# Attention values with a head's values stationary and normalised, turned probabilities moving

## The chip, the core and the metric

The kernel runs on one core of one Trainium2 chip. The time is device time in microseconds of one execution, and the figure of a kernel is the median of its runs. The engines are named as the profile names them: PE (matmuls; PEld is its weight load), DVE (vector), ACT (activation), POOL, and SP, which issues most transfers. A matmul holds one operand in the array (stationary) and streams the other through it (moving); its output goes to PSUM, which has eight banks of 128 partitions x 512 fp32 columns. DVE and ACT read PSUM and SBUF; POOL works in SBUF alone.

## The reference

Two layers of an encoder block on one sequence of 512 tokens of width 1024. Each layer is a half-weighted SwiGLU, a mixing part, a second half-weighted SwiGLU and a final norm. The mixing part projects the normed input once and splits the columns: one group is latent attention with 8 heads (queries and keys of 96, values of 64 per head, mask by chunks of 64 tokens), the other a gated causal convolution of 31 taps over 512 channels with a layer norm. Both are joined and projected back. What the change touches is this:

```
for i in range(s // Q_BLOCK):                       # Q_BLOCK = 128
    q0 = i * Q_BLOCK
    k_end = q0 + Q_BLOCK
    scores = einsum('bhqd,bhkd->bhqk', q[:, :, q0:k_end], k[:, :, :k_end]) * scale
    scores = where(k_chunk[None, :] <= q_chunk[:, None], scores, -1e30)
    probs = softmax(scores, axis=-1)
    outs.append(einsum('bhqk,bhkd->bqhd', probs, v[:, :, :k_end]))
x = x + concatenate([attn, conv], axis=-1) @ w_out
```

## The kernel before

The residual x lies in SBUF with features on partitions: eight tiles of 128 features x 512 tokens. The large products split each fp32 operand into a rounded high part and a low rest, and take three matmuls (`mm3`, L139 to L142) in place of one; `split` (L144) makes the two parts, the high one on ACT (L146), the low one on DVE (L147).

In `mix_body` the attention is cut into stages per head, and `ORDER = "t0s1p3v4o5"` gives each stage its lag in heads: at each step of the loop at L686 head h is turned (t), head h-1 scored (s), head h-3 has its probabilities turned (p), head h-4 its values taken (v), and head h-5 its output turned (o).

- `turn` (L604): queries and keys of a head, tokens on partitions, are transposed on PE to features on partitions, and copied out of PSUM by ACT (L609) and DVE (L614).
- `scores` (L617): for each of the four blocks of 128 queries one fp32 matmul against the 128, 256, 384 or 512 keys up to the block's end (L630), a small matmul that adds the mask (L631), the negated row maximum on DVE (L632), and the exponential on ACT (L636), which also adds up each row's sum. The probabilities are not divided by that sum here. They lie with queries on partitions, 1280 elements wide for a head over the four blocks.
- `turn_p` (L641): ten transposes on PE (L651) put keys on partitions; the results are copied to SBUF (L654), by DVE twice and by ACT once.
- `values` (L657): for each query block the turned probabilities are the stationary side (128 keys x 128 queries) and a head's 64 value columns move (L664): ten products per head, into a bank that two heads share by columns. Queries are on partitions, so the row sums are factors per partition: after the second head of a pair DVE takes reciprocals (L669) and multiplies the bank by them (L671) on the way to SBUF.
- `turn_out` (L675): four transposes on PE (L682) put the pair's 128 features on partitions, and `split` makes the operands of the output projection.

The convolution runs beside the attention, channels on partitions, in four tiles of 128 channels. For tiles of kind "D" DVE does all 30 shifted taps (L703) into a PSUM accumulator, which ACT copies out at the end (L713); for tiles of kind "A" ACT multiplies (L707) and POOL adds (L711). POOL then sums the four tiles (L725 to L727) for the layer norm's mean, PE spreads that sum (L729), and the first groups of the output projection follow (`early_groups`).

The order of the instructions on each engine is set when the program is built: a scheduler with its own estimate of durations deals the recorded instructions out to the engines, which then run them strictly in that order, each waiting on semaphores for its operands. So the convolution's taps stand between the attention's instructions where the scheduler has put them.

Of the kernel before, what the change touches and what calls it, by code (L numbers as in the profile page):

```python
# [7 lines left out]
FP = mybir.dt.float32  # L8
# [4 lines left out]
ALU = mybir.AluOpType  # L13
AX = mybir.AxisListType

P = 128
D = 1024
S = 512
L = 2
KD = D // P  # L20
NT = S // P
# [4 lines left out]
DV = 64  # L26
# [23 lines left out]
WOG = 3  # L50
WOP = 4
EVP = "DAD"
ORDER = "t0s1p3v4o5"

VECS = [("g1", 8), ("gm", 8), ("g2", 8), ("gp", 8), ("gql", 3), ("gkl", 2),
        ("cw", 4 * CK), ("cb", 4), ("lg", 4), ("lb", 4), ("gq", 1), ("gk", 1)]
# [11 lines left out]
def encoder_kernel(ctx: ExitStack, tc: tile.TileContext, xT, consts, vecs, rgain, wgu1, wd1,  # L68
# [8 lines left out]
    small = ctx.enter_context(tc.tile_pool(name="small", bufs=2))  # L77
# [3 lines left out]
    def nm(s):  # L81
        uid[0] += 1
        return f"{s}{uid[0]}"

    def slot(dt=FP, w=S):
        return ring.tile([P, w], dt, tag="r", name=nm("r"))

    def tmp(w=S, dt=FP):
        return tmps.tile([P, w], dt, tag="t", name=nm("t"))

    def bank():
        return psum.tile([P, S], FP, tag="ps", name=nm("ps"))
# [4 lines left out]
    V, A, G, T = nc.vector, nc.scalar, nc.gpsimd, nc.tensor  # L97
# [9 lines left out]
    ident = cst[:, CID:CID + P]  # L107
# [36 lines left out]
    def split(src, w=S):  # L144
        hi, lo = slot(FR, w), slot(FR, w)
        A.copy(hi, src)  # L146
        V.tensor_tensor(lo, src, hi.bitcast(FP), ALU.subtract)  # L147
        return hi, lo
# [40 lines left out]
    def spread(r):  # L189

        dg = tmp()
        V.tensor_tensor(dg.rearrange("p (t j) -> p t j", t=NT),
                        ident[:, None, :].to_broadcast([P, NT, P]),
                        r[:, :, None].to_broadcast([P, NT, P]), ALU.mult)
        ps = bank()
        T.matmul(ps, ones, dg, start=True, stop=True)
        return ps
# [214 lines left out]
    def mix(l, gx, norm, done):  # L412
        with tc.tile_pool(name="k", bufs=4) as kpool:
            mix_body(kpool, l, gx, norm, done)

    def mix_body(kpool, l, gx, norm, done):
# [25 lines left out]
        cqT, ckT, pq, scqs, vs = [], [], [], [], []  # L442
# [155 lines left out]
        at = []  # L598
# [3 lines left out]
        heads = [{} for _ in range(H)]  # L602
# [14 lines left out]
        def scores(h):  # L617
            qT, kT = heads[h]["qk"]
            b01, b2, b3 = bank(), bank(), bank()
            if h % 2 == 0:  # L620
                heads[h]["sums"] = small.tile([P, NT, 2], FP, tag="sums", name=nm("sums"), bufs=3)
            sums = heads[h - h % 2]["sums"]
            mx = small.tile([P, NT], FP, tag="mx", name=nm("mx"), bufs=3)
            pi = []
            ps = [slot() for _ in range(3)]
            ps = [ps[0][:, 0:128], ps[0][:, 128:384], ps[1][:, 0:384], ps[2]]
            for i in range(NT):
                n = (i + 1) * P
                o = (b01[:, 0:128], b01[:, 128:384], b2[:, 0:384], b3)[i]
                T.matmul(o, qT[0:DQ, i * P:(i + 1) * P], kT[0:DQ, 0:n], start=True, stop=False)  # L630
                heads[h]["s"] = T.matmul(o[:, n - 64:n], mrow, mneg, start=False, stop=True).ins  # L631
                V.tensor_reduce(mx[:, i:i + 1], o, axis=AX.X, op=ALU.max, negate=True)  # L632
                p = ps[i]
                if QFOLD:
                    V.tensor_tensor(mx[:, i:i + 1], mx[:, i:i + 1], scqs[i][:, h:h + 1], ALU.mult)
                A.activation(p, o, AF.Exp, bias=mx[:, i:i + 1], scale=scqs[i][:, h:h + 1] if QFOLD else 1.0,  # L636
                             accum_out=sums[:, i, h % 2:h % 2 + 1])
                pi.append(p)
            heads[h]["p"] = pi

        def turn_p(h):  # L641
# [15 lines left out]
        def values(h):  # L657

            if h % 2 == 0:
                heads[h]["po"] = bank()  # L660
            po = heads[h - h % 2]["po"].rearrange("p (t h d) -> p t h d", t=NT, h=2)
            for t in range(NT):
                for j in range(t + 1):
                    T.matmul(po[:, t, h % 2], heads[h]["pt"][j][:, (t - j) * P:(t - j + 1) * P],  # L664
                             vs[j][:, h * DV:(h + 1) * DV], start=j == 0, stop=j == t)
            if h % 2 == 0:
                return
            rs = small.tile([P, NT, 2], FP, tag="rs", name=nm("rs"))
            V.reciprocal(rs, heads[h - 1]["sums"])  # L669
            o = tmp()  # L670
            V.tensor_tensor(o.rearrange("p (t h d) -> p t h d", t=NT, h=2), po,  # L671
                            rs[:, :, :, None].to_broadcast([P, NT, 2, DV]), ALU.mult)
            heads[h]["o"] = o

        def turn_out(h):  # L675

            if h % 2 == 0:
                return
            o = heads[h]["o"]
            ps = bank()  # L680
            for t in range(NT):
                T.transpose(ps[:, t * P:(t + 1) * P], o[:, t * P:(t + 1) * P], ident)  # L682
            at.append(split(ps))

        STAGES = [({"t": turn, "s": scores, "p": turn_p, "v": values, "o": turn_out}[c], int(d)) for c, d in zip(ORDER[::2], ORDER[1::2])]
        for step in range(H + 6):  # L686
            for stage, lag in STAGES:
                if 0 <= step - lag < H:
# [6 lines left out]
        for c in range(4):  # L695
# [4 lines left out]
            for k in range(CK - 2, -1, -1):  # L700
                s = CK - 1 - k
# [41 lines left out]
        for c in range(4):  # L743
            z = tmp()
            V.tensor_tensor(z, ys[c], pr, ALU.mult)
            s = tmp()
# [53 lines left out]
    for l in range(L):  # L800
# [46 lines left out]
        else:  # L847
# [3 lines left out]
            ps = spread(st3.token(D))  # L851
            for m in range(KD):
                o = slot()
# [83 lines left out]
```

## Time and profile before

| | |
|---|---|
| median of 3 runs | 1857.76 us (1856.42 to 1858.85) |
| span of the profiled execution, first to last instruction | 1857.6 us |
| PE busy | 1816.5 us (98%) |
| DVE busy | 1353.9 us (73%) |
| ACT busy | 935.7 us (50%) |
| POOL busy | 341.5 us (18%) |
| mean granted TensorE clock | 0.991 of full |

The span is the profiled execution's own time from its first to its last instruction; the runs are timed apart from it. A share of busy time is a mean over stages that have different limits: the two attention stages, one a layer, are about 60 us each, and the rest of the span is mostly the feed-forward products. A duration in a row is the instruction's own, and instructions of one engine overlap at their ends; how long one holds its engine is the time from its start to the next one's. In a chain of what ended last, the second column is that share already.

### The profile page before, as it was taken

What the parts mean: (1) busy time and instruction counts of PE and PEld (TensorE: products, weight loads), DVE (VectorE), ACT (ScalarE), POOL (GpSimd) and SP (SyncE); (2) the same over time, 40 slices, a digit from 0 to 9 for tenths busy, and PEclk for the clock granted to TensorE, in tenths of its full rate; (3) what the DMA queues carried; (4) which work ended last, traced back from release to release, by engine and by line L of the source; (5) the groups of instructions that cost most, each with busy time, mean ns of one, the idle gap of its engine ahead of it and who ended that gap; (6) DMA issues with size and microseconds to landing.
All of it is one profiled execution on the core that took longest, in us unless ns stands there. A gap on an engine that the chain in (4) does not pass through costs nothing.

```text
span 1857.6 us, 27862 instructions
## 1 busy us (share of the span) xinstructions
PE 1816.5 (98%) x11240; PEld 1623.6 (87%) x11240; DVE 1353.9 (73%) x1761; ACT 935.7 (50%) x1467; POOL 341.5 (18%) x242
## 2 busy tenths in 40 slices
PE   7999999999899999999999999999999999999997
PEld 6898989888688898989888999898978788989895
DVE  5985858678855985858679767675989569767674
ACT  4453535457944453535634535354679435535351
POOL 3000000238924000000310000002589310000002
PEclk9999999999999999999999999999999999999998
DMA  6142422424213142423512414123250322424221
GB/s 217 41 142 69 135 68 91 122 74 125 46 58 110 39 140 77 128 77 94 165 54 63 150 55 148 57 87 114 78 148 1 108 80 63 142 63 143 63 86 63
DMA packets 55569, 175.72 MB, mean 95 GB/s; under 512 B 6160, under 2 KB 6544, under 8 KB 55440
## 3 DMA queue, kind: packets, MB, share of 16 engines
q1 hardware_dynamic: 53856, 169.37, 29.3%
q0 software_dynamic: 1152, 4.19, 1.3%
q8 instruction: 88, 1.44, 0.3%
q10 hardware_dynamic: 432, 0.38, 0.1%
q14 instruction: 41, 0.34, 0.1%
HBM read 171.82 MB, written 2.10 MB: 94 GB/s over the span
## 4 chain that ended last, share of the span: by engine, by line
PE 82%; DVE 7%; POOL 4%; ACT 4%; issue 3%; DMA 0%; POOLq 0%; ACTq 0%; DVEq 0%
PE ps L140 26%; PE ps L142 26%; PE ps L141 25%; PE ps L664 2%; PE ps L630 1%; ACT pr L707 1%; POOL y L711 1%; DVE wl L135 1%; POOL acc L173 1%; DVE r L283 1%; PE ps L651 1%; DVE cv L703 1%; DVE t L288 1%; POOL sck L158 1%; ACT wh L129 1%
## 5 line engine op out<-in xcount | busy, mean ns | idle before, releaser
L141 PE MATMUL ps<-r,wh 128*128 128x256 f32 (+1 forms) x3280 | 1060.7, 325 | 2.3 <-DVE r L153 2.2
L140 PE MATMUL ps<-r,wh 128*128 128x256 f32 (+1 forms) x3280 | 1053.7, 328 | 8.9 <-ACT wh L129 7.9
L142 PE MATMUL ps<-r,wl 128*128 128x256 f32 (+1 forms) x3280 | 1052.7, 325 | 3.9 <-DVE wl L135 1.9
L140 PEld LDWEIGHTS ps<-r,wh 128*128 128x128 f32 x3280 | 621.4, 191 | 64.8 <-ACT wh L129 8.7
L141 PEld LDWEIGHTS ps<-r,wh 128*128 128x128 f32 x3280 | 625.8, 191 | 55.1 <-DVE r L153 3.2
L142 PEld LDWEIGHTS ps<-r,wl 128*128 128x128 f32 x3280 | 622.2, 191 | 56.8 <-DVE wl L135 4.4
L223 ACT CAST wh<-fr 128x1024 fp32r<-128x1024 f32 x216 | 226.9, 1051 | 318.1 <-PE ps L141 233.0
L129 ACT CAST wh<-raw 128x768 fp32r<-128x768 f32 (+4 forms) x214 | 187.7, 883 | 337.5 <-PE ps L141 170.0
L173 POOL TENSOR_TENSOR acc<-acc,t 128x512 f32<-128x512 f32 x52 | 89.4, 1725 | 1308.5 <-ACT t L172 1307.4
L225 DVE TENSOR_TENSOR wl<-fr,wh 128x1024 fp32r<-128x1024 f32 x216 | 263.8, 1222 | 79.6 <-ACT wh L223 76.6
L135 DVE TENSOR_TENSOR wl<-raw,wh 128x768 fp32r<-128x768 f32 (+4 forms) x198 | 209.5, 1063 | 125.9 <-ACT wh L129 124.5
L399 DVE SCALAR_TENSOR_TENSOR x<-ps,x 128x512 f32<-128x512 f32 x128 | 87.6, 687 | 119.1 <-PE ps L142 119.1
L711 POOL TENSOR_TENSOR y<-y,pr 128x509 f32<-128x509 f32 (+15 forms) x120 | 157.5, 1313 | 51.9 <-ACT pr L707 44.6
L703 DVE SCALAR_TENSOR_TENSOR cv<-r,vec,cv 128x511 f32<-128x511 f32 (+14 forms) x120 | 87.7, 731 | 3.1 <-ACT cv L699 1.7
L707 ACT ACTIVATE pr<-r,vec 128x511 f32<-128x511 f32 (+14 forms) x120 | 83.5, 722 | 8.2 <-POOL y L711 8.0
L223 ACT CAST wh<-raw 128x1024 fp32r<-128x1024 f32 x36 | 37.7, 1047 | 70.3 <-PE ps L141 70.3
L146 ACT CAST r<-t 128x512 fp32r<-128x512 f32 x96 | 55.7, 620 | 33.5 <-DVE t L260 20.6
L147 DVE TENSOR_TENSOR r<-t,r 128x512 fp32r<-128x512 f32 x96 | 64.7, 686 | 10.2 <-ACT r L146 10.2
L225 DVE TENSOR_TENSOR wl<-raw,wh 128x1024 fp32r<-128x1024 f32 x36 | 44.1, 1225 | 30.9 <-ACT wh L223 30.9
L630 PE MATMUL ps<-r,r 96*128 96x384 f32 (+3 forms) x128 | 47.8, 492 | 8.6 <-ACT r L609 4.4
L336 DVE TENSOR_TENSOR raw<-fr,fr 128x1024 f32<-128x1024 f32 x36 | 44.0, 1223 | 12.9 <-DMA fr<-in_wgu 12.9
L153 DVE SCALAR_TENSOR_TENSOR r<-x,vec,r 128x512 fp32r<-128x512 f32 x40 | 45.9, 1148 | 10.2 <-ACT r L152 10.2
(165 smaller groups left out, 1596.4 us busy)
## 6 DMA issues: line engine op xcount, KB each, us to landing
fr<-in_wgu SPq DMA_DIRECT2D x144, 512.0 KB, 3.6
raw<-in_wd SPq DMA_DIRECT2D x96, 384.0 KB, 3.1
raw<-in_wgu SPq DMA_DIRECT2D x32, 512.0 KB, 3.5
raw<-in_wd SPq DMA_DIRECT2D x32, 256.0 KB, 2.6
raw<-in_wcv SPq DMA_DIRECT2D x16, 512.0 KB, 3.6
raw<-in_wout SPq DMA_DIRECT2D x16, 512.0 KB, 4.5
wl<-in_wout POOLq DMA_DIRECT2D x8, 512.0 KB, 6.7
raw<-in_wql SPq DMA_DIRECT2D x6, 512.0 KB, 3.5
```

Source lines behind the costliest of these rows:

```text
L129: A.copy(hi[:, :w], raw[:, :w])
L135: (G if kind in POOLW.split() else V).tensor_tensor(lo[:, :w], raw[:, :w], hi[:, :w].bitcast(FP), ALU.subtract)
L140: T.matmul(o, lh, rh, start=first, stop=False, skip_group_check=free)
L141: T.matmul(o, lh, rl, start=False, stop=False, skip_group_check=free)
L142: T.matmul(o, ll, rh, start=False, stop=last, skip_group_check=free)
L173: (eng or (V if last else G)).tensor_tensor(self.acc, self.acc, sq, ALU.add)
L223: A.copy(hi[:, :w], src[:, :w])
L225: V.tensor_tensor(lo[:, :w], src[:, :w], hi[:, :w].bitcast(FP), ALU.subtract)
L399: V.scalar_tensor_tensor(x[:, m, :], pd, 0.5, x[:, m, :], ALU.mult, ALU.add)
L703: V.scalar_tensor_tensor(acc[:, s:], u[c][:, :S - s], tap(k), acc[:, s:], ALU.mult, ALU.add)
L707: A.activation(pr[:, s:], u[c][:, :S - s], AF.Copy, scale=tap(k))
L711: order["conv"] = G.tensor_tensor(acc[:, s:], acc[:, s:], pr[:, s:], ALU.add).ins
```

## The change

The division by the row sum moves to the front: right after a head's exponentials DVE takes the reciprocals of its four columns of sums (now one tile a head, no longer one a pair) and multiplies each of the four blocks of probabilities in place, in SBUF. Then the probabilities are turned as before. In `values` the roles are swapped: a head's 64 value columns of a key block are the stationary side, and the turned, normalised probabilities of that key block move, all query columns from the block's own to the last. The output has features on partitions: the first head of a pair writes partitions 0 to 63 of a bank, the second 64 to 127, in turns over the four key blocks. This is the layout that the output projection wants, so the multiplication on the way out, the stage `turn_out` and its four transposes per pair go, and `split` reads the bank at once. Nothing is done for the first head of a pair when its turn comes; both heads' products are issued at the second's.

```diff
-ORDER = "t0s1p3v4o5"
+ORDER = "t0s1p3v4"
...
-            if h % 2 == 0:
-                heads[h]["sums"] = small.tile([P, NT, 2], FP, tag="sums", name=nm("sums"), bufs=3)
-            sums = heads[h - h % 2]["sums"]
+            sums = small.tile([P, NT], FP, tag="sums", name=nm("sums"), bufs=3)
+            rs = small.tile([P, NT], FP, tag="rs", name=nm("rs"), bufs=3)
...
-                             accum_out=sums[:, i, h % 2:h % 2 + 1])
+                             accum_out=sums[:, i:i + 1])
                 pi.append(p)
+            V.reciprocal(rs, sums)
+            for i in range(NT):
+                V.tensor_scalar(pi[i], pi[i], rs[:, i:i + 1], None, ALU.mult)
             heads[h]["p"] = pi
...
             if h % 2 == 0:
-                heads[h]["po"] = bank()
-            po = heads[h - h % 2]["po"].rearrange("p (t h d) -> p t h d", t=NT, h=2)
-            for t in range(NT):
-                for j in range(t + 1):
-                    T.matmul(po[:, t, h % 2], heads[h]["pt"][j][:, (t - j) * P:(t - j + 1) * P],
-                             vs[j][:, h * DV:(h + 1) * DV], start=j == 0, stop=j == t)
-            if h % 2 == 0:
                 return
-            rs = small.tile([P, NT, 2], FP, tag="rs", name=nm("rs"))
-            V.reciprocal(rs, heads[h - 1]["sums"])
-            o = tmp()
-            V.tensor_tensor(o.rearrange("p (t h d) -> p t h d", t=NT, h=2), po,
-                            rs[:, :, :, None].to_broadcast([P, NT, 2, DV]), ALU.mult)
-            heads[h]["o"] = o
-
-        def turn_out(h):
-
-            if h % 2 == 0:
-                return
-            o = heads[h]["o"]
-            ps = bank()
-            for t in range(NT):
-                T.transpose(ps[:, t * P:(t + 1) * P], o[:, t * P:(t + 1) * P], ident)
-            at.append(split(ps))
+            po = bank()
+            for j in range(NT):
+                for e in (0, 1):
+                    T.matmul(po[e * DV:(e + 1) * DV, j * P:S], vs[j][:, (h - 1 + e) * DV:(h + e) * DV],
+                             heads[h - 1 + e]["pt"][j], start=j == 0, stop=j == NT - 1)
+            at.append(split(po))
```

Where the instructions stand is shown at three places of the first layer. Names are tiles: `mx` row maxima, `rs` reciprocals, `cv` the convolution accumulator in PSUM, `ps` a PSUM bank, `r` a tile of the ring in SBUF (probabilities, turned probabilities and values all lie there); the text ends with the output's partitions x elements.

DVE, around the turned copies of the second head, before:

```order
L654 COPY r_4616<-ps_4615 128x512
L654 COPY r_4630<-ps_4629 128x256
L703 SCALAR_TENSOR_TENSOR cv_5263<-r_4428,vec,cv_5263 128x497
L632 TENSOR_REDUCE mx_4595<-ps_4592 128x1
L703 SCALAR_TENSOR_TENSOR cv_5263<-r_4428,vec,cv_5263 128x496
L614 TENSOR_SCALAR r_4657<-ps_4652,vec 96x512
```

and now, where the scalings of the third head stand ahead of the same copies:

```order
L638 RECIPROCAL rs_4552<-sums_4551 128x4
L631 TENSOR_REDUCE mx_4616<-ps_4613 128x1
L688 SCALAR_TENSOR_TENSOR cv_5231<-r_4428,vec,cv_5231 128x499
L640 TENSOR_SCALAR r_4554<-r_4554,rs_4552 128x128
L640 TENSOR_SCALAR r_4554<-r_4554,rs_4552 128x256
L640 TENSOR_SCALAR r_4555<-r_4555,rs_4552 128x384
L640 TENSOR_SCALAR r_4556<-r_4556,rs_4552 128x512
L656 COPY r_4642<-ps_4641 128x512
L656 COPY r_4656<-ps_4655 128x256
L631 TENSOR_REDUCE mx_4616<-ps_4611 128x1
```

Each head has such a block of four scalings in a row, 32 a layer, among the convolution's taps, and the taps move later: the last one stood ahead of the copies of the sixth head, and stands behind those of the eighth now.

PE, the values of a pair. Before, a head's ten products, among them:

```order
L664 MATMUL ps_4634<-r_4200,r_4560 128x64 x2
L664 MATMUL ps_4634<-r_4227,r_4567 128x64
L664 MATMUL ps_4634<-r_4200,r_4560 128x64
L664 MATMUL ps_4634<-r_4227,r_4567 128x64
L664 MATMUL ps_4634<-r_4254,r_4574 128x64
```

and now both heads' products in one run:

```order
L666 MATMUL ps_4723<-r_4579,r_4200 64x512
L666 MATMUL ps_4723<-r_4642,r_4200 64x512
L666 MATMUL ps_4723<-r_4586,r_4227 64x384
L666 MATMUL ps_4723<-r_4649,r_4227 64x384
L666 MATMUL ps_4723<-r_4593,r_4254 64x256
L666 MATMUL ps_4723<-r_4656,r_4254 64x256
L666 MATMUL ps_4723<-r_4586,r_4281 64x128
L666 MATMUL ps_4723<-r_4649,r_4281 64x128
```

Twenty products with 64 moving columns have become eight with 128 to 512, in turns for the two heads.

DVE at the end of the attention, before:

```order
L671 TENSOR_TENSOR t_4956<-ps_4905,rs_4954 128x512
L654 COPY r_4959<-ps_4958 128x512
L654 COPY r_4973<-ps_4972 128x256
L147 TENSOR_TENSOR r_4994<-ps_4988,r_4993 128x512
L671 TENSOR_TENSOR t_5009<-ps_4977,rs_5007 128x512
L147 TENSOR_TENSOR r_5017<-ps_5011,r_5016 128x512
```

and now:

```order
L656 COPY r_4957<-ps_4956 128x512
L656 COPY r_4971<-ps_4970 128x256
L688 SCALAR_TENSOR_TENSOR cv_5231<-r_4428,vec,cv_5231 128x483
L688 SCALAR_TENSOR_TENSOR cv_5231<-r_4428,vec,cv_5231 128x482
L147 TENSOR_TENSOR r_4985<-ps_4975,r_4984 128x512
```

The last two taps have moved behind the last copies; on ACT the copy of their accumulator (L713 before, L698 now) stands behind the cast of the last pair's split.

More of the change, by code (lines that the diff above doesn't have):

```diff
@@ L659, in values @@
             if h % 2 == 0:
-                heads[h]["po"] = bank()
-            po = heads[h - h % 2]["po"].rearrange("p (t h d) -> p t h d", t=NT, h=2)
-            for t in range(NT):
-                for j in range(t + 1):
-                    T.matmul(po[:, t, h % 2], heads[h]["pt"][j][:, (t - j) * P:(t - j + 1) * P],
-                             vs[j][:, h * DV:(h + 1) * DV], start=j == 0, stop=j == t)
-            if h % 2 == 0:
-                return
-            rs = small.tile([P, NT, 2], FP, tag="rs", name=nm("rs"))
-            V.reciprocal(rs, heads[h - 1]["sums"])
-            o = tmp()
-            V.tensor_tensor(o.rearrange("p (t h d) -> p t h d", t=NT, h=2), po,
-                            rs[:, :, :, None].to_broadcast([P, NT, 2, DV]), ALU.mult)
-            heads[h]["o"] = o
-        def turn_out(h):
-            if h % 2 == 0:
-                return
-            o = heads[h]["o"]
-            ps = bank()
-            for t in range(NT):
-                T.transpose(ps[:, t * P:(t + 1) * P], o[:, t * P:(t + 1) * P], ident)
-            at.append(split(ps))
-        STAGES = [({"t": turn, "s": scores, "p": turn_p, "v": values, "o": turn_out}[c], int(d)) for c, d in zip(ORDER[::2], ORDER[1::2])]
+                return
+            po = bank()
[4 more added lines that the diff above has]
+            at.append(split(po))
+        STAGES = [({"t": turn, "s": scores, "p": turn_p, "v": values}[c], int(d)) for c, d in zip(ORDER[::2], ORDER[1::2])]
         for step in range(H + 6):
```

## The prediction

> **What bounds the kernel now.** I read the page first, then the two attention stages (about 470 to 531 us in the first layer, 1385 to 1445 us in the second): busy times by stretch, the chain that ended last inside them, and the order of time on DVE and POOL. From the page (busy us, share, instructions):
>
> ```profile
> span 1857.6 us, 27862 instructions
> PE 1816.5 (98%) x11240; PEld 1623.6 (87%) x11240; DVE 1353.9 (73%) x1761; ACT 935.7 (50%) x1467; POOL 341.5 (18%) x242
> ```
>
> PE bounds the whole, but the change lives in the attention stages, and there the shares are others. Stretches of them (start:end, length, busy us and instructions of each engine, then the granted clock):
>
> ```profile
> core 0: us, PE busy (x) PEld busy (x) DVE busy (x) ACT busy (x) POOL busy (x), PEclk, DMA share, GB/s
> 487.00:500.00 13.00, 12.75 (x95) 10.71 (x96) 12.34 (x25) 13.00 (x35) 12.22 (x10) 1.00 0.01 2
> 500.00:513.00 13.00, 13.00 (x99) 10.86 (x98) 12.55 (x26) 12.26 (x30) 12.28 (x10) 1.00 0.00 1
> 513.00:518.00 5.00, 5.00 (x37) 3.86 (x35) 5.00 (x11) 4.83 (x13) 4.70 (x4) 1.00 0.00 0
> 518.00:531.20 13.20, 12.41 (x111) 12.13 (x111) 5.49 (x11) 3.49 (x9) 3.93 (x4) 1.00 0.01 1
> ...
> 1413.00:1426.00 13.00, 13.00 (x99) 10.83 (x97) 12.88 (x26) 12.59 (x31) 12.27 (x10) 1.00 0.00 1
> ```
>
> Until 518 us PE, DVE, ACT and POOL are all within a few per cent of full: DVE is idle 0.66 + 0.45 + 0 us in 31. Only after 518 us has DVE room, 7.7 us. The second layer's row reads the same. The chain (start, us, engine and line) shows which of the full engines ends last:
>
> ```profile
> 499.88 0.49 PE ps L630 x2
> 501.29 0.22 PE ps L630 x2
> 501.54 0.73 PE ps L630 x2
> 502.30 0.94 PE ps L630 x2
> 504.40 2.18 PE ps L664 x20
> 507.10 0.47 PE ps L682 x4
> 529.87 0.70 DVE t L671
> 530.61 0.65 PE ps L682 x4
> ```
>
> It is PE row after row, with one step of DVE at the very end. So time taken from PE is worth something here only as long as DVE, nearly as full, does not grow.
>
> **The change on PE.** Removed per layer: eight times L664 at 2.18 us (an fp32 product is two instructions in the trace, so a head's ten products are x20), 17.4 us, and four times L682 at 0.47, 1.9 us: 19.3 together. Added for each head: four products with 512, 384, 256 and 128 moving columns. The fp32 scores L630 move just these widths: 0.94 + 0.73 + 0.49 + 0.22 = 2.38 us a head, 19.0 us a layer, if the array's two halves are used one after the other. No row shows products in different halves side by side; at best they cost half, 9.5 us, and PE sheds 9.8 us a layer. I take 19.0, by the nearest rows, and count PE's change (-0.3 us) as nothing. The Trainium skill, "TensorEngine Tiling (Array Packing)", Theoretical Speedup, puts a stationary side of at most 64 at up to 2x, which no run here shows; by that PE sheds the 9.8 us, and whether it shows in the time hangs on DVE.
>
> **The change on DVE, its own work.** Each head gets a reciprocal and four in-place scalings of 128, 256, 384 and 512 elements; each pair loses one L671 and its reciprocal. The prices: two copies of 512 and 256 elements up to the next start; L671 up to the next start; the smallest in-place scaling by a per-partition factor (L544, 8 elements) up to the next start; the reciprocals, with their mean in ns:
>
> ```profile
> 513.48 1.01 DVE L654 COPY r<-ps 128x512 f32<-128x512 f32 x2
> 514.41 0.72 DVE L703 SCALAR_TENSOR_TENSOR cv<-r,vec,cv 128x482 f32<-128x482 f32 x1
> 523.96 0.69 DVE L671 TENSOR_TENSOR t<-ps,rs 128x512 f32<-128x512 f32 x1 [0.74 <-PE ps L664]
> 524.57 1.01 DVE L654 COPY r<-ps 128x512 f32<-128x512 f32 x2
> ...
> 433.30 0.22 DVE L544 TENSOR_SCALAR ssh<-ssh,cq 128x8 f32<-128x8 f32 x1
> 433.43 0.54 DVE L542 TENSOR_REDUCE ssh<-t 128x4 f32<-128x384 f32 x1
> ...
> L669 DVE RECIPROCAL rs<-sums 128x8 f32<-128x8 f32 x4 | 0.8, 192 | 0.6 <-ACT r L636 0.6
> ```
>
> The copies hold DVE 0.93 us for 768 elements, so 1280 elements cost 1.55 us a head, 12.4 us a layer. The lower end is L544's 0.13 us for each of 32, 4.2 us. I take 12.4: the copies have the size, L544 hardly any data. Removed: 4 x 0.61 = 2.4. Four more reciprocals: at most 4 x 0.19 = 0.8. Own work: +10.8 us a layer (lower end +2.6). The Trainium skill, "VectorE: DVE Perf Modes", The perf-mode tier table, lets a scaling from SBUF to SBUF run fp32 at twice the rate that a PSUM operand allows; no row here shows one of size. By it the scalings would be 6.2 us, and the forecast near 1885 instead of 1898 us.
>
> **The change on DVE, its waits.** L544 is the same kind of instruction as the new scalings: in place in SBUF, with a factor per partition. Alone it took 0.22 us. Beside POOL's L711, and so its kin L578 and the two-input L581 (0.42 us alone), it did not:
>
> ```profile
> 427.16 2.60 POOL L711 TENSOR_TENSOR y<-y,pr 128x498 f32<-128x498 f32 x2
> 428.72 1.07 DVE L544 TENSOR_SCALAR ssh<-ssh,cq 128x8 f32<-128x8 f32 x1
> ...
> 449.75 0.42 DVE L581 TENSOR_TENSOR kn<-ck,scp 128x256 f32<-128x256 f32 x1
> ...
> 454.98 2.30 DVE L578 TENSOR_SCALAR scp<-sck,ratio 128x8 f32<-128x8 f32 x1 [1.53 <-POOL sck L158]
> 455.68 1.57 POOL L711 TENSOR_TENSOR y<-y,pr 128x496 f32<-128x496 f32 x1
> 457.20 0.68 DVE L579 TENSOR_TENSOR kn<-kn,sck 128x512 f32<-128x512 f32 x1
> 457.33 1.67 POOL L711 TENSOR_TENSOR y<-y,pr 128x495 f32<-128x495 f32 x1
> 457.80 1.48 DVE L581 TENSOR_TENSOR kn<-ck,scp 128x256 f32<-128x256 f32 x1
> ```
>
> L544 ended at 429.79, when POOL's pair did (429.76); L578 at 457.28, as POOL's 457.25. L579 slipped in before POOL's next, which then took 1.67 us, and L581 waited 1.06 us for that one. So they take turns. In the attention stage POOL runs one L711 after another, while L632, L654, L671 and L703 with a PSUM operand keep their lengths; before the change nothing of this kind stands there on DVE.
>
> ```profile
> 477.62 40.54 POOL L711 TENSOR_TENSOR y<-y,pr 128x511 f32<-128x511 f32 x31 [0.29 <-ACT pr L707]
> ...
> 1404.95 30.09 POOL L711 TENSOR_TENSOR y<-y,pr 128x504 f32<-128x504 f32 x23 [0.37 <-ACT pr L707]
> ```
>
> A turn of POOL is 40.54 / 31 = 1.31 us. Bounds of the waits: none, or 32 x 1.31 = 41.9 us a layer. My value: of a head's four scalings one slips in behind another, as L579 did, so three meet POOL. POOL has 12.22 + 12.28 + 4.70 + 3.93 = 33.1 us of work after 487 us; in a stage grown from 44 to some 64 us that is a share of 0.52. Who meets a turn midway waits half of it, who finds one queued all of it: about 1.0 us. 24 x 0.52 x 1.0 = 12.5 us. What stands behind the waiting scalings on DVE are the next head's maxima, which ACT's exponentials wait for, and copies of turned probabilities, which PE's values wait for; so the wait reaches both. POOL in turn is held by at most 12.4 us of scalings; the longer stage leaves it idle time for that, else its last sum moves by as much.
>
> **The room, and the sum.** DVE's idle time after 487 us is 8.8 us (above). But the new end needs part of it. Its steps: the last pair's values (2 x 2.38 = 4.8 us); then ACT's L146; behind it in ACT's order the copy of the last convolution accumulator, whose DVE taps now stand after the last turned copies; POOL's last sum; and only then PE's L729, which starts the next part:
>
> ```profile
> 515.36 0.58 ACT L713 COPY r<-cv 128x512 f32<-128x512 f32 x1
> 520.81 1.27 POOL L727 TENSOR_TENSOR t<-t,r 128x512 f32<-128x512 f32 x1
> 527.68 0.58 ACT L146 CAST r<-ps 128x512 fp32r<-128x512 f32 x1 [2.26 <-PE ps L682]
> 531.11 1.02 PE L729 MATMUL ps<-t,onesm 128*128 128x512 f32 x2
> ```
>
> That is 4.8 + 0.58 + 0.58 + 1.27 = 7.2 us, in which DVE works about 1.9 us (two taps, one split) and idles 5.3. Room: 8.8 - 5.3 = 3.5 us. The sum a layer: 10.8 + 12.5 - 3.5 = +19.8 us, with DVE in PE's place as the bound. Behind the stage PE is dense, so both layers' delays reach the end: 1857.6 + 39.6 = 1897, rounded up to 1898 us. The span of the profiled execution is the runs' median (1857.76) within 0.2 us. No DMA is moved and no queue changes its order.
>
> **Rivals.**
> - DVE grows, but the scalings do not wait for POOL (against it: the two rows that did): 10.8 - 3.5 = 7.3 us a layer, 1872 us.
> - Every scaling waits a whole turn: 10.8 + 41.9 - 3.5 = 49.2 us a layer, 1956 us. It needs POOL's next tap always ready; against it, the taps come through ACT's order, which itself waits for DVE.
> - Faster: the scalings cost near L544's 0.13 us and do not wait, so DVE's +2.6 stays under the room of 3.5 us, PE stays the bound, and the two halves work side by side. PE then sheds 9.8 us a layer: 1838 us. The point that decides is DVE's growth against 3.5 us; with halves one after another it ends at no change. For it speaks the chain, all PE; against it the waits above.
>
> **The numbers.** Forecast 70 in 100, no waits 14, whole turns 8, faster 8 (with one or two of these at no change). 0.2% is about what a measurement can tell from none. Faster 0.07, same 0.03, slower 0.90. The range: low with +2.6 of own work and 5.2 us of waits (+4.3 a layer), 1866; high with all 32 meeting POOL at eight in ten of a turn (33.5 us, +40.8 a layer), 1939. About one in ten lies beyond each.
>
> **What would show it.** Scalings at L640 longer than 0.5 us and ending with a POOL tap; POOL taps above 1.31 us; the attention stage some 80 us long instead of 61, with DVE or its waits on the chain where PE stood; pairs of values near 4.8 us (half of it: the halves run together). I am wrong if scalings last 0.2 to 0.5 us beside running taps, or if PE is still dense there.

## The result and the profile after

The changed kernel took 1878.39 us (median of 4 runs, 1874.6 to 1879.35) beside 1858.30 us of the kernel before on the same chip: 1.0104 times as long, 95% interval 1.009 to 1.0119. It is slower, as forecast and within the range, but by 20 us where the forecast said 40.

The first lines of the page after (span, then busy us, share of the span and instructions of each engine):

```profile
span 1876.3 us, 27478 instructions
PE 1819.1 (97%) x11016; PEld 1601.5 (85%) x11016; DVE 1384.1 (74%) x1825; ACT 937.5 (50%) x1467; POOL 343.6 (18%) x242
```

DVE works 30 us more than before over the whole span. PE has 224 instructions less, yet 2.6 us more of busy time. The stretches of the first layer's attention, in the columns of the prediction's table, show why these two go together:

```profile
470.00:487.00 17.00, 14.77 (x63) 9.03 (x64) 16.00 (x28) 15.07 (x35) 16.12 (x14) 0.80 0.25 58
487.00:500.00 13.00, 12.95 (x55) 8.97 (x54) 13.00 (x26) 10.49 (x25) 11.22 (x9) 0.64 0.00 0
500.00:513.00 13.00, 11.70 (x73) 7.41 (x73) 13.00 (x29) 12.66 (x33) 10.96 (x10) 1.00 0.01 2
513.00:523.00 10.00, 8.19 (x50) 4.67 (x48) 10.00 (x22) 7.35 (x20) 9.29 (x8) 1.00 0.00 0
523.00:531.00 8.00, 5.91 (x20) 2.73 (x20) 7.37 (x20) 1.72 (x5) 0.81 (x1) 0.57 0.01 3
531.00:539.00 8.00, 5.43 (x36) 3.15 (x33) 5.26 (x9) 4.18 (x7) 1.26 (x1) 1.00 0.00 0
```

From 487 to 523 us DVE is never idle: 36.0 us of 36. PE now has gaps (1.3 us from 500, 1.8 us from 513, 2.1 us from 523), and where it has none, from 487 to 500, it does 55 instructions where it did 95: its granted clock is 0.64 there, and 0.57 from 523. So DVE took PE's place. The chain between 470 and 545 us says the same; its summary by line, before and then after:

```profile
by line: PE ps L664 23.3%; PE ps L630 16.1%; PE ps L651 10.3%; ACT pr L707 9.0%; ACT r L636 4.9%; PE ps L140 3.8%; PE ps L142 3.7%; PE ps L141 3.6%; ACT r L609 3.1%; issue 2.8%; PE ps L682 2.7%; PE ps L612 2.6%; PE ps L607 1.8%; POOL y L711
```

```profile
by line: DVE cv L688 19.3%; DVE r L640 17.6%; DVE mx L631 16.1%; PE ps L666 10.5%; DVE r L656 6.9%; DVE r L614 5.3%; PE ps L653 4.6%; PE ps L629 3.0%; issue 2.8%; PE ps L140 2.4%; PE ps L142 2.1%; PE ps L141 2.1%; POOL t L712 1.7%; DVE r L1
```

L640 are the new scalings. In the order of time on DVE, a head's four scalings stand in one row (start, us, and x4; the shape named is the first one's). Five of the eight heads of layer 0:

```profile
483.25 3.46 DVE L640 TENSOR_SCALAR r<-r,rs 128x128 f32<-128x128 f32 x4
...
494.67 3.60 DVE L640 TENSOR_SCALAR r<-r,rs 128x128 f32<-128x128 f32 x4
...
503.32 1.26 DVE L640 TENSOR_SCALAR r<-r,rs 128x128 f32<-128x128 f32 x4
504.50 0.41 DVE L656 COPY r<-ps 128x256 f32<-128x256 f32 x1
...
516.61 2.22 DVE L640 TENSOR_SCALAR r<-r,rs 128x128 f32<-128x128 f32 x4
...
524.77 1.26 DVE L640 TENSOR_SCALAR r<-r,rs 128x128 f32<-128x128 f32 x4
```

The same 1280 elements take 1.26 us or up to 3.60 us. The 1.26 us at 503.32 fall into a gap in POOL's row, and at 524.77 POOL's taps are over; the 3.60 us lie beside a run of taps that is itself stretched to 10.29 / 7 = 1.47 us a tap, from 1.31 before. POOL's order of time:

```profile
490.39 10.29 POOL L696 TENSOR_TENSOR y<-y,pr 128x503 f32<-128x503 f32 x7 [1.23 <-ACT pr L692]
500.87 2.64 POOL L696 TENSOR_TENSOR y<-y,pr 128x496 f32<-128x496 f32 x2 [0.19 <-ACT pr L692]
504.58 2.56 POOL L696 TENSOR_TENSOR y<-y,pr 128x494 f32<-128x494 f32 x2 [1.07 <-ACT pr L692]
```

On PE, the turns wait for these scalings (groups over both layers: busy us, mean ns, then idle time in front and what ended it), before and after:

```profile
L651 PE MATMUL ps<-cst,r 128*128 128x128 f32 x160 | 20.6, 274 | 0.3 <-ACT r L636 0.3
```

```profile
L653 PE MATMUL ps<-cst,r 128*128 128x128 f32 x160 | 28.1, 316 | 11.8 <-DVE r L640 7.8 <-ACT r L635 3.0 <-DVE r L656 0.6
```

The part that the forecast had not counted stands in PE's order of time, the values of a pair of heads:

```profile
500.61 2.38 PE L666 MATMUL ps<-r,r 128*64 128x512 f32 x16
502.92 0.70 PE L629 MATMUL ps<-r,r 96*128 96x256 f32 x2
```

Both heads' eight products (x16, two instructions each) are done in 2.31 us up to the next start. The forecast had 4.8 us, before it was 4.4. The two partition halves run side by side.

The end of the stage runs as its steps were listed, the last values, the split's cast, the copy of the accumulator, POOL's sum, then L714 (L729 before):

```profile
533.19 3.20 PE L666 MATMUL ps<-r,r 128*64 128x512 f32 x16
...
536.43 0.59 ACT L146 CAST r<-ps 128x512 fp32r<-128x512 f32 x1 [2.65 <-PE ps L666]
...
536.91 0.59 ACT L698 COPY r<-cv 128x512 f32<-128x512 f32 x1
...
537.64 1.26 POOL L712 TENSOR_TENSOR t<-t,r 128x512 f32<-128x512 f32 x1 [13.83 <-ACT r L698]
...
538.96 1.13 PE L714 MATMUL ps<-t,onesm 128*128 128x512 f32 x2 [2.57 <-POOL t L712]
```

L714 starts at 538.96 us, 7.85 us behind L729 before; in the second layer at 1463.76, where L729 stood at 1445.19, which makes 18.6 us. That is the growth of the span (18.7 us). It arises in the two attention stages, here from the first product of the scores to the start of L729 or L714 (both layers before, then both layers after, in the columns above):

```profile
471.61:531.11 59.50, 57.55 (x401) 46.58 (x402) 49.75 (x96) 48.84 (x118) 47.52 (x39) 0.95 0.07 16
1387.85:1445.19 57.34, 55.90 (x401) 45.63 (x401) 49.49 (x96) 48.00 (x118) 47.27 (x39) 0.97 0.06 13
```

```profile
470.16:538.96 68.80, 58.91 (x289) 35.91 (x289) 64.47 (x129) 51.28 (x121) 49.51 (x39) 0.83 0.06 14
1394.06:1463.76 69.70, 59.01 (x289) 35.56 (x289) 65.23 (x129) 50.40 (x120) 48.29 (x39) 0.85 0.04 8
```

The stages grow by 9.3 and 12.4 us, to some 69 us and not to the 80 that were forecast. DVE works 14.7 and 15.7 us more in them and is idle 5.4 and 3.4 us less. Of these 21.7 us some 3 come back outside: the first stage starts 1.5 us earlier than before, and the second starts 6.2 us late, where the first had ended 7.85 us late.

### The profile page after: what moved, and what is told of

It is laid out like the page before. It is cut to its first block, busy times and chain, and to the rows that moved or that the text cites. A ratio compares the mean times of both kernels' runs of the same rounds, so it can differ in the third digit from the quotient of the medians.

```text
span 1876.3 us, 27478 instructions
## 1 busy us (share of the span) xinstructions
PE 1819.1 (97%) x11016; PEld 1601.5 (85%) x11016; DVE 1384.1 (74%) x1825; ACT 937.5 (50%) x1467; POOL 343.6 (18%) x242
## 4 chain that ended last, share of the span: by engine, by line
PE 78%; DVE 12%; ACT 3%; POOL 3%; issue 3%; DMA 0%; POOLq 0%; ACTq 0%; DVEq 0%
PE ps L140 25%; PE ps L142 25%; PE ps L141 25%; DVE cv L688 2%; DVE r L640 1%; DVE mx L631 1%; DVE wl L135 1%; POOL y L696 1%; DVE r L283 1%; ACT pr L692 1%; PE ps L666 1%; DVE t L288 1%; ACT wh L129 1%; POOL acc L173 1%; DVE r L656 1%
## 5 line engine op out<-in xcount | busy, mean ns | idle before, releaser
L688 DVE SCALAR_TENSOR_TENSOR cv<-r,vec,cv 128x511 f32<-128x511 f32 (+14 forms) x120 | 87.7, 731 | 3.2 <-ACT cv L684 1.7
L629 PE MATMUL ps<-r,r 96*128 96x384 f32 (+3 forms) x128 | 53.3, 541 | 10.4 <-ACT cv L684 4.1
```

What stands on the lines that cost most here:

```text
L688: V.scalar_tensor_tensor(acc[:, s:], u[c][:, :S - s], tap(k), acc[:, s:], ALU.mult, ALU.add)
```

## The experiments

The theory after the result: the growth is a sum of two parts of opposite sign, the scalings in DVE's full stretch with their waits for POOL, and a relief of PE by the new values, which the forecast had put at nothing. The rival theories: the low clock of PE is what costs; or only one of the two parts matters and its size was wrong. Times stand beside the kernel before as it ran in the same batch. Its medians in the batches lie between 1857.2 and 1859.0 us, so a difference between kernels of two batches is uncertain by 1 to 2 us; of each kernel one execution was profiled.

**The new values alone.** The changed kernel without its normalisation.

```diff
-            V.reciprocal(rs, sums)
-            for i in range(NT):
-                V.tensor_scalar(pi[i], pi[i], rs[:, i:i + 1], None, ALU.mult)
```

> The changed kernel without the reciprocals and the scalings: its attention output is not divided by the row sums. Theory (DVE with its new work ends the attention stage): without that work the swapped values help, since PE sheds some 10 us a layer; the stage is then held by DVE, ACT and POOL with 49 to 51 us of work each in place of PE's 57.6, so 4 to 9 us a layer come back: 1840 to 1850 us. Rival (the new form of the values costs by itself, by idle PE and a lower granted clock): 1858 us or more.

Measured: 1846.61 us beside 1858.97, ratio 0.9939 (0.9922 to 0.9955). With no scaling on DVE the new values, with L671 and the turns of the outputs gone, are worth 12.4 us, which is inside the theory's range. It is the lowest time of all the kernels here, and no normalisation is in it.

**The scalings alone.** The kernel before, its old values kept, but normalised in front as in the changed kernel; L671 becomes a plain copy.

```diff
+            V.reciprocal(rs, sums)
+            for i in range(NT):
+                V.tensor_scalar(pi[i], pi[i], rs[:, i:i + 1], None, ALU.mult)
...
-            V.tensor_tensor(o.rearrange("p (t h d) -> p t h d", t=NT, h=2), po,
-                            rs[:, :, :, None].to_broadcast([P, NT, 2, DV]), ALU.mult)
+            V.tensor_copy(o.rearrange("p (t h d) -> p t h d", t=NT, h=2), po)
```

> The kernel before with the scalings in front and the old values: the multiplication on the way out becomes a plain copy. Theory (DVE ends the stage): PE's 10 us saved by the swapped values were not worth anything beside the scalings, so about the changed kernel's time plus four copies of 0.6 us a layer: 1876 to 1890 us. Rival (the saving on PE is already in the +20 us): 1895 to 1902 us.

Measured: 1897.47 us, ratio 1.0206 (1.0183 to 1.0229). The theory's range is missed and the rival's holds: the scalings cost 38.5 us when PE keeps its old work. So going from here to the changed kernel, which takes away about half of the products' time, the turns of the outputs and L671, gives 19.1 us back. The stages of this kernel, in the same columns, show where from:

```profile
468.48:549.32 80.84, 69.65 (x401) 55.78 (x402) 70.66 (x132) 49.91 (x118) 49.30 (x39) 0.83 0.05 12
1405.54:1479.73 74.19, 64.20 (x401) 50.01 (x402) 66.45 (x132) 49.21 (x118) 50.18 (x39) 0.89 0.04 10
```

They are 16.5 us longer in both layers than those of the changed kernel. DVE works 7.4 us more in them (the copies at L671, longer waits), and it is idle 17.9 us where it is idle 8.8 in the changed kernel. By what ended the idle time, 11.4 of the 17.9 us were waits for PE's products, and 3.1 of the 8.8. So PE's work is on the path even in a stage that DVE nearly fills. Towards the end of the first stage it stands there plainly, at a clock of 0.65 (the stretch, and a head's ten products, 2.18 us before):

```profile
526.00:539.00 13.00, 10.74 (x51) 9.81 (x52) 10.16 (x24) 4.95 (x16) 0.00 (x0) 0.65 0.00 0
...
531.81 4.37 PE L666 MATMUL ps<-r,r 128*128 128x64 f32 x20
```

**Without POOL's turns.** The changed kernel, and as its control the kernel before, with all of the convolution's additions on POOL but the last of each chain left out.

```diff
                     G.tensor_scalar(pr[:, s:], u[c][:, :S - s], tap(k), None, ALU.mult)
+                if k > 0:
+                    continue
```

> The changed kernel with all but the last of POOL's convolution adds left out (two of the four channel tiles are then wrong). Theory (DVE's scalings wait for POOL's turns, 7 to 8 us a layer): the scalings take 1.26 us a head throughout and 12 to 16 us come back: 1862 to 1867 us. Rival (only the scalings' own work costs; waits fall into idle time): within 3 us of the changed kernel, 1875 to 1881 us.

> The kernel before with the same adds left out, as a control. Theory (PE ends the stage): 1854 to 1861 us. Rival (POOL's chain helps to set the end): below 1850 us.

Measured: 1867.03 us (ratio 1.0045, 1.003 to 1.006), at the upper edge of the theory's range, and 1869.81 us (ratio 1.0061, 1.0046 to 1.0076). The control missed: it should have fallen or stayed, and it rose by 10.8 us. In both, the instructions of DVE and ACT stand in another order than in the kernel they are compared with. So the 11.4 us between the changed kernel and its variant can't be read as the price of the waits. What the pair does give is the scalings' undisturbed price, and by it the waits. The group of L640, both layers, first without POOL's taps, then in the changed kernel, and then with the old values:

```profile
L640 DVE TENSOR_SCALAR r<-r,rs 128x128 f32<-128x128 f32 (+1 forms) x64 | 20.2, 378 | 0.0
```

```profile
L640 DVE TENSOR_SCALAR r<-r,rs 128x128 f32<-128x128 f32 (+1 forms) x64 | 35.5, 615 | 0.0
```

```profile
L640 DVE TENSOR_SCALAR r<-r,rs 128x128 f32<-128x128 f32 (+1 forms) x64 | 38.7, 664 | 0.0
```

20.2 us without taps, 10.1 a layer; 35.5 with them, so the waits are 15.3 us, 7.7 a layer.

**The halves one after the other.** The changed kernel with the two loops of the values swapped: all products of the first head, then all of the second. Nothing else is edited.

```diff
-            for j in range(NT):
-                for e in (0, 1):
+            for e in (0, 1):
+                for j in range(NT):
```

> The changed kernel with a pair's products no longer in turns: four of the first head, then four of the second. Theory now (the scalings cost what was forecast, and the two halves side by side give it partly back): a pair's values take 4.4 to 4.8 us in place of 2.3 and the time rises by 8 to 18 us, 1886 to 1896. Rival (DVE alone ends the stage, PE's time counts only in its tail): 1878 to 1883 us. If the pair stays at 2.3 us, the order does not decide whether halves run together, and the time stays.

Measured: 1887.61 us (1882.55 to 1890.33) beside 1857.80, ratio 1.015 (1.0128 to 1.0171), 9.2 us above the changed kernel and in the theory's range. A pair now takes 3.85 us instead of 2.31, at a clock of 1.00 in both:

```profile
500.92 3.93 PE L666 MATMUL ps<-r,r 128*64 128x512 f32 x16
504.77 0.70 PE L629 MATMUL ps<-r,r 96*128 96x256 f32 x2
```

The eight pairs of both layers lose 1.54 us each, 12.3 us. How the 9.2 us come about is not shown. Every engine has the same instructions, but some of DVE's and ACT's stand in another order. The profiled execution is the fastest of the four (1882.55 us, which the rival's range would hold), 4.4 us longer than that of the changed kernel, and its two stages hold 1.6 us of this:

```profile
470.48:539.12 68.64, 58.73 (x288) 35.64 (x289) 64.03 (x129) 51.29 (x121) 49.37 (x39) 0.93 0.06 13
1394.17:1465.67 71.50, 61.37 (x280) 37.30 (x281) 67.14 (x128) 50.78 (x120) 49.15 (x39) 0.86 0.05 12
```

DVE is idle 9.0 us in them, no more than in the changed kernel, and PE's mean clock in the first is 0.93 where it was 0.83, which can have hidden a part. So the order of the loops decides how long a pair takes; what that is worth in time is shown by the medians alone. That 3.85 us are less than the forecast's 2 x 2.38 = 4.76 us for products one after another means that something still overlaps in this order; what, was not followed further.

**PE's clock.** Six products of a zero bf16 tile ahead of each head's turns keep PE busy where it waited.

```diff
+    idle = cpool.tile([P, S], BF, name="idle")
+    V.memset(idle, 0.0)
...
             for js, eng in (((0,), EVP[0]), ((1, 3), EVP[1]), ((2,), EVP[2])):
                 ps = bank()
                 sb = slot()
+                for _ in range(2):
+                    T.matmul(ps, mrow, idle, start=True, stop=True)
```

> The changed kernel with six idle bf16 matmuls of 512 columns (zeros, results overwritten) ahead of each head's transposes of probabilities, where PE waits for the scalings: some 10 us of PE work a layer. Theory (the granted clock falls to 0.6 where PE waits, and the work after it runs at that clock): the clock reads 0.95 or more in each stretch and the time does not rise, 1868 to 1878 us. Rival (the low clock costs nothing, PE's extra work does): 1882 to 1898 us.

Measured: 1877.10 us beside 1857.80, ratio 1.0098 (1.0082 to 1.0114), the changed kernel's time, and in the theory's range. The two stretches of the first layer in which the clock was 0.64 and 0.57 have it at 1.00 now:

```profile
487.00:500.00 13.00, 11.02 (x63) 6.89 (x62) 13.00 (x28) 10.88 (x25) 11.31 (x10) 1.00 0.00 1
...
526.00:539.00 13.00, 12.08 (x61) 5.66 (x59) 9.68 (x23) 5.87 (x13) 1.27 (x1) 1.00 0.00 0
```

In the second layer two stretches still have 0.87 and 0.74, so 0.95 in each was not reached. Where PE is kept busy in its waits, then, the clock is higher. What the low clock costs stays open. The 96 idle products take some 0.22 us each, 21 us of PE in both layers, and the time did not rise, where the rival had it rise. Either they fell into waits, or the higher clock paid for them; the two stages of the profiled execution take 134.3 us where the changed kernel's take 138.5. What is shown is that raising the clock in this way does not bring the time down.

**Other places for the normalisation.** Four kernels keep the new values and move the scaling. First, exponentials left in PSUM, and the scalings read from there:

```diff
-                p = ps[i]
+                p = o
...
-                V.tensor_scalar(pi[i], pi[i], rs[:, i:i + 1], None, ALU.mult)
-            heads[h]["p"] = pi
+                V.tensor_scalar(ps[i], pi[i], rs[:, i:i + 1], None, ALU.mult)
+            heads[h]["p"] = ps
```

> The changed kernel with the exponentials written over the scores in PSUM, so that the scalings read PSUM and not SBUF; POOL's work stays. Theory (an instruction with a PSUM operand does not wait for POOL): scalings take 0.65 us at 512 elements and 1.6 us a head throughout, none longer; waits of 7 to 8 us a layer go, 3 us of work come: 1866 to 1873 us. Rival (the banks, held longer, stop PE): 1878 us or more, with scalings still free of waits.

Measured: 1912.46 us beside 1857.80, ratio 1.0286 (1.027 to 1.0302). Theory and rival were each right in part. Not one scaling waits, with POOL at work as before (lengths in ns: least, median, most), but the scores' banks stay taken until the scaling is done, PE's scores wait for banks (4.9 us of waits for the scalings), and PE does 32 instructions from 487 to 500 us where the changed kernel does 55:

```profile
L640 DVE TENSOR_SCALAR r<-ps,rs x64: 344/542/744, 482.0 to 1486.4; 128x128 f32<-128x128 f32 x16, 128x256 f32<-128x256 f32 x16, 128x384 f32<-128x384 f32 x16, 128x512 f32<-128x512 f32 x16
...
487.00:500.00 13.00, 7.67 (x32) 4.88 (x33) 12.96 (x28) 10.82 (x24) 12.22 (x11) 0.74 0.00 0
```

Second, ACT takes the blocks of 384 and 512 elements:

```diff
             for i in range(NT):
+                if i >= 2:
+                    A.activation(pi[i], pi[i], AF.Copy, scale=rs[:, i:i + 1])
+                    continue
                 V.tensor_scalar(pi[i], pi[i], rs[:, i:i + 1], None, ALU.mult)
```

> The changed kernel with the two wide scalings of each head (384 and 512 elements) on ACT, the two narrow ones on DVE. Theory (DVE's work and its waits for POOL set the growth; ACT has room once DVE is late): DVE sheds some 5 us a layer of work and about half its waits, ACT takes on 8 us: 1862 to 1872 us. Rival (ACT is as full as DVE, its convolution products then come late for POOL): 1878 us or more.

Measured: 1864.49 us beside 1857.80 (10 runs, 1861.76 to 1867.6), ratio 1.0034 (1.0022 to 1.0046): 13.9 us below the changed kernel, as the theory had it, and still above the kernel before.

Third, nothing is scaled in front. The reciprocals are laid on a diagonal, products with ones spread them over the free axis of a bank, again in halves, and one product per pair normalises the values. Fourth, the same with the diagonal written by ACT.

```diff
-            for i in range(NT):
-                V.tensor_scalar(pi[i], pi[i], rs[:, i:i + 1], None, ALU.mult)
+            dg = tmp()
+            V.tensor_tensor(dg.rearrange("p (t j) -> p t j", t=NT), ident[:, None, :].to_broadcast([P, NT, P]),
+                            rs[:, :, None].to_broadcast([P, NT, P]), ALU.mult)
...
+                pR = bank()
+                for e in (0, 1):
+                    T.matmul(pR[e * DV:(e + 1) * DV], ones[:, 0:DV], heads[h - 1 + e]["dg"], start=True, stop=True)
+                o = tmp()
+                A.copy(o, pR)
...
+            V.tensor_tensor(o, o, po, ALU.mult)
+            at.append(split(o))
```

> The changed kernel with its turned values left as they are (both heads in one bank's partition halves), but the 64 scalings of the probabilities of a layer taken out. In their place the reciprocals of a head's sums are spread on a diagonal (one DVE product of 128x512 per head), a product with ones lays them along the free axis for both heads side by side in one bank, ACT copies that bank, and one DVE product of 128x512 per pair normalises the values. Nothing of the computation is left out. Theory (the growth is the scalings: their own time of 1.2 us per head and their waits of 0.9 us per head on a DVE that became the bound, set against a PE that sheds about 10 us per layer): DVE now spends per pair two products of about 0.6 us and one of 0.6 instead of about 4.3, some 2.5 us less per pair or 10 per layer; PE spends about 1 us more per pair, 4 per layer. Time 1852 to 1866, between the 1846.6 of the kernel without any normalising and the 1878.4 of the changed kernel, and about that of before. Rival (any further work on DVE, or a further bank held, costs what the scalings cost): 1870 to 1885.

> As the kernel with the normalising behind the values, but the diagonal is written by ACT in four pieces of 128x128 per head (about 0.37 us each, 1.5 us per head) instead of by DVE in one product. Theory (DVE is what counts in the changed kernel): DVE loses another 0.6 us per head, 5 per layer, ACT has room for 12 us more per layer as it had for 11 when it took the wider scalings: 1846 to 1862, at or below the sibling. Rival (ACT's own chain of exponentials and evacuations feeds PE, so work there is as dear): 4 us or more above the sibling.

Measured: 1865.98 us beside 1857.16, ratio 1.0047 (1.0035 to 1.0059), at the upper end of the theory's range and below the rival's; and with ACT's diagonal 1867.93 us, ratio 1.0062 (1.005 to 1.0074), which neither had: 2 us above the sibling, where the theory wanted it at or below and the rival 4 above. DVE's diagonals, with two operands in SBUF, again meet POOL now and then (least, median, most in ns):

```profile
L640 DVE TENSOR_TENSOR t<-cst,rs x16: 675/726/1684, 482.0 to 1443.5; 128x512 f32<-128x512 f32 x16
```

So less work on DVE helps by 12 to 14 us and then stops, and taking the rest from DVE to ACT helps no more: in the fourth kernel's first stage ACT is busy 61.05 of 64.08 us, and DVE 51.88. No full normalisation tried here came under the kernel before.

## Why the prediction was right in sign and wrong in size

Its mechanism held on DVE's side: the scalings fill DVE, they take turns with POOL's taps, DVE comes onto the chain in PE's place, and the end of the stage goes through the steps that were listed. The size was twice what came. By the terms of the sum, in us a layer:

| term | forecast | measured, and where |
|---|---|---|
| PE's products, counted as nothing | 0 | a pair 2.31 us, not 4.8, so PE sheds 4 x 2.5 = 10 us; it shows in DVE's idle time (room, below) |
| scalings, own time | 12.4 | 10.1 (20.2 us in both layers, without taps) |
| waits for POOL | 12.5 | 7.7 (15.3 us in both layers) |
| four more reciprocals | 0.8 | 0.6 at most: 8 x 0.08 us up to the next start |
| L671 and its reciprocals gone | -2.4 | not measured apart |
| these together, DVE's work in a stage | 23.3 | 15.2 (14.7 and 15.7 us in the stages) |
| room, DVE's idle time that is used up | -3.5 | -4.4 (5.4 and 3.4 us in the stages) |
| outside the stages | 0 | -1.5 (2.9 us in both layers) |
| sum, against the growth | 19.8 | 9.4 in the profiled executions (18.7 us), 10.0 in the medians (20.1 us) |

A stage is as long as DVE's work and idle time in it, so the lower rows add up by construction; what they show is how much of the growth is work. Two terms of the sum failed by their size. The waits, "24 x 0.52 x 1.0 = 12.5 us", measured 7.7, and the scalings, 12.4, measured 10.1. By the stages DVE's work was forecast 8.1 us a layer too high, 7.1 of it in these two, and that is most of the miss of 9.8 us.

The third step that failed is "I take 19.0, by the nearest rows, and count PE's change (-0.3 us) as nothing". The row it went by, the scores of the same widths, uses a stationary side of 128 columns; it could not show what two halves do. The prediction had the other end, 9.8 us less a layer, and let it matter only if DVE's growth stayed under 3.5 us. DVE's growth was far over that, and yet the new values as a whole are worth 12.4 us in both layers without scalings and 19.1 us beside them. The stages show the way. With the scalings in front and the old values DVE is idle 9.0 us a layer, as much as before (8.8): there is no room at all. With the new values it is idle 4.4 us. So the room comes with the new values, where the forecast put PE's change at nothing and read the room off the end of the stage (7.2 us there, 5.3 of them idle; measured 5.8 and 2.6 in the first layer). That its 3.5 us lie near the measured 4.4 is luck. Two engines that feed each other head by head are not bound by the fuller one alone: each waits for the other in turn.

Against the Trainium skill, "TensorEngine Tiling (Array Packing)", Theoretical Speedup, which gives up to 2x for a stationary side of at most 64: the runs show 3.85 / 2.31 = 1.67 between products of one half at a time and products in turns.

The scalings' own time was read from copies out of PSUM (0.93 us for 768 elements). From SBUF they are cheaper. From 128x128 to 128x512 they take 277 to 478 ns from SBUF, in the changed kernel without taps, and 348 to 742 ns from PSUM, in the kernel with the exponentials left there (means):

```profile
L640 DVE TENSOR_SCALAR r<-r,rs 128x512 f32<-128x512 f32 x16 | 7.7, 478 | 0.0
...
L640 DVE TENSOR_SCALAR r<-r,rs 128x128 f32<-128x128 f32 x16 | 4.4, 277 | 0.0
```

```profile
L640 DVE TENSOR_SCALAR r<-ps,rs 128x512 f32<-128x512 f32 x16 | 11.9, 742 | 0.0
...
L640 DVE TENSOR_SCALAR r<-ps,rs 128x128 f32<-128x128 f32 x16 | 5.6, 348 | 0.3
```

That is (478 - 277) / 384 = 0.52 ns an element from SBUF and 1.03 from PSUM. The Trainium skill, "VectorE: DVE Perf Modes", The perf-mode tier table, gives just this factor of two (with its part on PSUM operands), and the runs agree. The time that an instruction takes whatever its length, about 0.21 us by these rows, keeps the saving at 2.3 us a layer where the page's factor alone would have made it 6.2, by an estimate.

The waits were right in kind and 4.8 us a layer too long. The forecast had 24 x 0.52 = 12.5 scalings a layer wait 1.0 us each. Set against their lengths without taps, 21 of the 64 scalings waited, 10.5 a layer, and 0.73 us on average: 13 waited a whole turn (0.96 to 1.04 us) and 8 only a part of one (0.14 to 0.54 us). Each of the 21 ends just behind the end of one of POOL's instructions, by 0.08, 0.15, 0.22 or 0.28 us for the four widths. Of the other 43, which kept the lengths without taps, 25 met no running instruction of POOL (for at most a tenth of their length), and only 4 ran beside one all along. The heads of layer 0 show waits of 0 (three heads) to 2.3 us (3.60 - 1.26); summed they are 7.3 us. Of the three heads without a wait one fell into a gap in which POOL itself waited for ACT (1.07 us at 504.58), two came after the taps. The Trainium skill, "SBUF — State Buffer", Who interferes with whom, holds that whichever of the two comes first keeps the port for its whole instruction; the lengthened taps (1.47 us) beside the lengthened scalings (up to 1.48 us where 0.48 is usual) agree with it, and so do the scalings out of PSUM, which never waited (344 to 744 ns).

The rows for DVE's work can be held against the stages. Scalings, waits and reciprocals less L671 make 10.1 + 7.7 + 0.6 - 2.4 = 16.0 us a layer, where DVE's work grew by 15.2. In the kernel with the scalings alone, which keeps a copy at L671, they make 10.1 + 9.25 + 0.6 = 20.0, where DVE's work grew by 18.9; its idle time grew by 0.2, and the kernel's time by 19.2. So the sizes hold to about 1 us a layer. Each account rests on one profiled execution, and the two layers of one differ by up to 7 us. What the halves side by side give apart from the rest of the new values stays open, and so does what the low clock costs.

Of the rivals, "no waits" fell, since the waits are 7.7 us a layer, though its 1872 us are nearer to the result than the forecast; it came nearer for a wrong reason. "Whole turns" fell with waits of 15.3 us in 64 scalings. "Faster" had the halves right and the scalings wrong, and the kernel without scalings shows what it rested on: 1846.6 us, not 1838.

## What to carry to other kernels

Two operations on 64 stationary columns each can share the array if their products are issued in turns; all of one and then all of the other loses more than half of the gain (3.85 us a pair, between 2.31 and 4.76), so look at the order of the loops: here it changed a pair by 1.54 us and the median time by 9 us. Before an operation is moved onto an engine, look at what else is full in that stretch: a scaling of the [128x1280] probabilities in front cost 38.5 us here, while all that it saved behind was worth 19.1. And when two engines are both over 95% busy and feed each other, count the relief of the one even where the other is to grow: look for it in the other's idle time.

## What the runs showed of the hardware that was not expected

- Fp32 products with 64 stationary columns in alternating halves of a bank's partitions: eight (two each of 512, 384, 256 and 128 moving columns) in 2.31 us, 3.85 us when the halves follow one another.
- A single-source scaling in SBUF and a two-source product in SBUF on DVE both take turns with POOL's additions (up to 1.48 us where 0.48 is usual, and up to 1.68 us where 0.73 is); reciprocals of 4 elements never did (157 to 169 ns), nor did DVE's instructions with an operand in PSUM (the taps at L688 697 to 755 ns).
- PE's granted clock fell to 0.64 and 0.57 in stretches around its waits for DVE. Six products of zeros per head (128x512, bf16) held it at 1.00 in these stretches of the first layer, and the time did not change.
